# A decoder layer on one core: the third tile's convolution taps move behind the norm of the second output projection, and two weights of the first tile are loaded into a free buffer

## The chip, the core and the metric

The kernel runs on 1 core of one Trainium2 chip. The metric is the time of one execution in microseconds on the device, the median of several runs. Before the change it is 1910.04 us (3 runs, 1907.92 to 1913.49).

The engines go by the profile's names: PE (TensorE, matmuls; PEld is its weight load), DVE (VectorE), ACT (ScalarE), POOL (GpSimd) and SP (SyncE, which issues most DMAs).

## The reference

One hybrid decoder layer, float32, 2048 tokens, width 1024:

```
hn   = rms_norm(x) ; proj = hn @ w_in          # q, k, v and the two halves of a GLU
attn = sliding window attention (window 128, sinks, relative bias)
u    = a * sigmoid(gate)
conv = silu(layer_norm(depthwise causal conv of width 31 (u))) @ w_conv_pw
h    = x + rms_norm(concat(attn, conv) @ w_out)
out  = h + rms_norm((silu(hn2 @ w_gate) * (hn2 @ w_up)) @ w_down),  hn2 = rms_norm(h)
```

## The kernel before

The tokens are cut into 4 tiles of 512 (t = 0 to 3). A float32 product is made as three matmuls of split operands: every operand is a high half, made by a copy on ACT, and a low half, operand minus high half, made by a subtraction on DVE. `split_w` (L130) does this for weights, `split_f` and `lo` for the FFN. A matmul with 512 columns is the unit of PE's work; 24 of them make one unit of the input projection, 12 one product of the FFN.

The stages are generators:

- `stage_a(t)` is the input projection of a tile, in units of 128 output columns. In the first tile units 0 to 3 go together (`four`), and the norm's factor `rb` is multiplied in behind the product (`post`). Units come in GLU pairs (0/1, 2/3, 4/5, 6/7), then k (8), v (9) and q (10 to 13). `proj(u)` loads the weight of unit u through `kweight` (L146) and `weight` (L140) into a tile tagged "raw" (2 buffers; L143 is the load), splits it into two "w" tiles (6 buffers; L133 is the ACT copy, the low half is a DVE subtraction) and runs 24 matmuls. `glu` makes tanh on ACT (L377), the products on DVE, and in the first tile one more multiply by `rb`, on POOL for the first pairs (L385), then stores to `glu_scr`.
- `row_norms` loads the rows of x of the next tile (L276, tag "p"), squares them on ACT (L277) and makes their factors on DVE and POOL.
- `stage_taps(t)`, lane items T0 to T3, is the convolution: 4 channel groups, each loaded from `glu_scr` (L594, L596), one first multiply and 30 taps on DVE (`fc@C<-glu@C,colt,fc@C` in the profile), stored to `y_scr` (L621).
- `stage_b(t)` is the attention of a tile: scores (`tr@B<-kz,ql@A`), masking and row maxima on DVE (L493, L496), exponentials on ACT, transposes and the product with v.
- `stage_w(w)` is the output projection of a tile, for w = 0 and 1 as 32 pieces of 6 matmuls (`mm@W<-w@W,hl@W`); operands `hl@W` are split on ACT (L785) and DVE. `norm_w` is its norm and residual. For w = 1 it is handed to a lane as the item "N1".
- `stage_h_plain` and `stage_h_sums` ("S0") make the FFN's operands, `stage_pre` the first part of the first FFN matrices (products P0.0, P0.1, ...), `stage_p1` the rest and `stage_p2` the down projection. The last two are a Strassen-like scheme of 7 products for 8.

The main sequence is `run(...)` of one stage after another. After every piece of it, `run` lets the lanes emit side work: each lane earns credit (the piece's cost times the lane's rate) and spends it on the costs its generators yield. `lc` is the lane of the taps: T2 has the rate RC2 = 0.4, and each tap costs 0.68. `lh` is the lane of B11.0, B21.0, N1 and S0, at 1.2 for N1. `lc.hold` is a function; while it is true, the lane emits nothing. A tap is also tied behind the last DVE instruction of the main work (`paced`), and its lane has a lower priority (LC = 100). Below this, a planner orders the instructions of each engine by readiness in a timeline of its own and by priority, which is by default the order of emission; buffers of a tag are handed on when their last reader is done. On the chip each engine runs its list in that order.

Before the change T2 is emitted beside `stage_w(1)`, and from the end of `stage_w(1)` the hold is on until S0 is done (S0 starts at product P0.22, `PRE_S0`). The tile "yt" (one buffer of 128 x 2048 float32) is used by the weight join (`stage_join`, from the third tile on), by `stage_tail` and in the FFN; nothing uses it in the first tile.

Of the kernel before, what the change touches and what calls it, by code (L numbers as in the profile page):

```python
# [25 lines left out]
P = 128  # L26
T = 512
# [10 lines left out]
def layer_kernel(ctx, tc, x, xT, cols, rows, sinks, relb, onehot, w_in, w_four, w_pw, w_out, w_gate, w_up, w_down, out):  # L38
    nc = tc.nc
# [9 lines left out]
    def nm(s):  # L49
        uid[0] += 1  # L50
        return f"{s}@{lab[0]}_{uid[0]}"
# [3 lines left out]
    def t_(tag, shape, dt=F32):  # L55
        return sb.tile(list(shape), dt, tag=tag, name=nm(tag), bufs=BUFS[tag])

    def f4(tag, shape=(P, D)):
        return t_(tag, shape)

    def f2(tag, shape=(P, T)):
        return t_(tag, shape)

    def hl(tag):
        return t_(tag, (P, 2, T), F32R)
# [5 lines left out]
    def bank(tag, bufs):  # L71
        return ps.tile([P, T], F32, tag=tag, name=nm(tag), bufs=bufs)

    mm = lambda: bank("mm", 4)
# [65 lines left out]
    def weight(src, low, made, raw=None, on_pool=True):  # L140
        if raw is None:
            raw = t_("raw", (P, 2, T))
            nc.sync.dma_start(raw, src)  # L143
        return [split_w(raw[:, n], "w", low[n], made, on_pool) for n in range(2)]

    def kweight(u, made, raw=None):  # L146
        hs = weight(w_in[u].rearrange("p (a b) -> p a b", a=2), lo_in[u], made, raw, False)
        return [(hs[k // 4][:, 0, (k % 4) * P : (k % 4 + 1) * P], hs[k // 4][:, 1, (k % 4) * P : (k % 4 + 1) * P]) for k in range(KC)]
# [41 lines left out]
    def three(o, pairs, first=True, last=True):  # L190
        n = 3 * len(pairs)
        i = 0
        for (sh, sl), (mh, ml) in pairs:
            for a, b in ((sh, mh), (sh, ml), (sl, mh)):
                mat(o, a, b, start=first and i == 0, stop=last and i == n - 1)
                i += 1
# [58 lines left out]
    started = set()  # L255
# [60 lines left out]
    def split_x(t, xs, rb, ks):  # L316
# [12 lines left out]
            hn.append(hk)  # L329
        return hn  # L330

    def stage_a(t, hn, done_with, hooks, post=None):
        L = f"A{t}"
        lab[0] = L
        rb = None

        def proj(u, bank_of=mm):
            w = kweight(u, t > 0)
            o = bank_of()
            for k in range(KC):  # L340
                three(o, [(w[k], (hn[k][:, 0], hn[k][:, 1]))], k == 0, k == KC - 1)
            return o
# [64 lines left out]
        done_with("S")  # L407
        lab[0] = L
        ok = proj(8)
        if t:  # L410
            act(kz[:, :, 0:P], kz[:, :, T : T + P].bitcast(F32), AF.Copy)
# [212 lines left out]
    def stage_tail(t, sink=None):  # L624
        L = f"C{t}"
        lab[0] = L
        yt = t_("yt", (P, 4, 4 * P))
        ycs = []
        turn = turner(yt, ycs)
        for c in range(4):  # L630
            lab[0] = L
            y = f2("fc")
            nc.sync.dma_start(y, y_scr[c, :, t * T : (t + 1) * T])
            ycs.append(y)
            turn(c)
            yield 0.5
        yield from conv_tail(t, yt, sink)
# [34 lines left out]
    def spare_tile():  # L672
        if not spare:
            spare.append(t_("mb", (P, 2, T)))
        return spare[0]
# [76 lines left out]
    def block_half(acc, units, n, first, L, bank_of, s0=0):  # L752
        cs = slice(n * T, (n + 1) * T)
        for i in range(len(acc)):
            s = i + s0
            lab[0] = L
            o = bank_of()
            three(o, [((a[s // 4][:, 0, ss(s)], a[s // 4][:, 1, ss(s)]), (w[:, 0], w[:, 1])) for a, w in units])
            if first:
                act(acc[i][:, cs], o, AF.Copy)  # L760
            else:
                vtt(acc[i][:, cs], acc[i][:, cs], o, ALU.add)
            yield 0.65 * len(units)

    def load_gb(row):
        gb = []
        for n in range(2):
            t = f2("gb")
            nc.sync.dma_start(t, rows[row, n * T : (n + 1) * T].partition_broadcast(P))
            gb.append(t)  # L770
        return gb
# [6 lines left out]
    def stage_w(w, spill, G, atag, htag, mtag, bank_of, norm=None):  # L778
        L = f"W{w}"
        lab[0] = L  # L780
        acc = [f4(atag) for _ in range(4)]

        def operand(m):
            a = hl(htag)
            act(a[:, 0], m, AF.Copy)  # L785
            vtt(a[:, 1], m, a[:, 0].bitcast(F32), ALU.subtract)
            return [a]

        def acts(gi, ms=None):
            return [operand(m) for m in ms or load(gi)]  # L790

        conv = []
        tail = stage_tail(w, lambda v: conv.append(operand(v))) if w > 1 else ()
        for y in tail:
            if y == YL2:
                break
            yield y
        lab[0] = L

        stage = spare_tile() if w == 1 else None  # L800

        def load(gi):
            ms = []
            pair_ = stage if w == 1 else t_("chl", (P, 2, T)) if w else t_("wx", (P, 2, T)) if gi == 0 else None
            for c in range(G * gi, G * gi + G):
                ms.append(pair_[:, c % 2] if pair_ is not None else f2(mtag))
                nc.sync.dma_start(ms[-1], mixT[c, :, w * T : (w + 1) * T])
            return ms

        first = load(0)  # L810
        gb = load_gb(0) if w > 1 else None
        if w != 1:
            yield 5.0 if w == 0 else 8.0
            lab[0] = L
        nxt = acts(0, first)
        for gi in range(KC // G):
            if w > 1 and G * gi == 4:
                yield from tail
                lab[0] = L
            aa = nxt if w < 2 or G * gi < 4 else conv[G * gi - 4 : G * gi - 4 + G]  # L820
            for n in range(2):
                lab[0] = L
                more = gi + 1 < KC // G and (w < 2 or G * gi + G < 4)
                if n == 0 and more:
                    if w < 2 and G * gi + G == 4:
                        ld.until(f"C{w}")
                        lab[0] = L
                    rows_next = load(gi + 1)
                if n == 1 and more:
                    nxt = acts(gi + 1, rows_next)  # L830
                src = w_out[2 * gi : 2 * gi + 2] if gi < 2 else w_join[2 * gi - 4 : 2 * gi - 2]
                ws = weight(src[:, :, n * T : (n + 1) * T].rearrange("c p t -> p c t"),
                            lo_out[n, 2 * gi : 2 * gi + 2], w > 0, on_pool=False)
                yield from block_half(acc, list(zip(aa, ws)), n, gi == 0, L, bank_of)
        last = norm_w(w, spill, acc, mtag, gb)
        if norm:
            norm(last)
        else:
            yield from last
# [381 lines left out]
    def stage_p2(ws, am, td, last=False):  # L1221
# [34 lines left out]
        def split(i):  # L1256
            if i < len(steps):
                lab[0] = L
                b = split_f(rawb[i], hl(("ql" if i >= len(steps) - 4 else "w") if last else "hl"))
                lo(rawb.pop(i), b, False)  # L1260
                if last and i == len(steps) - 2:
                    rest.append(t_("yt", (P, 2, 2, T), F32R))
                a = split_f(rawa[i], rest[0][:, i % 2] if last and i >= len(steps) - 2 else hl("hl"))
                lo(rawa.pop(i), a, False)
                opsd[i] = a, b
# [79 lines left out]
        for i in range(nn):  # L1345
# [3 lines left out]
            if i + N < nn + (LAST > 0):  # L1349
                split(i + N)  # L1350
            if last and nn - EARLY - 3 <= i < nn - EARLY + LAST - 4:
                load(i + EARLY + 4)
            if last and nn - EARLY <= i < nn - EARLY + LAST - 1:
                split(i + EARLY + 1)
            for b in range(4):
# [33 lines left out]
    def since(lane, name, dt):  # L1389
        return name in lane.done and clk[0] >= lane.done[name] + dt  # L1390
# [66 lines left out]
    PRE_S0, PRE_S2 = 22, 16  # L1457
    H1, H2, H3, H4 = 0, 4, 7, 11
    NH = 24
    EARLY = 12  # L1460
    JL, JS = 10, 2
    lb = Lane(RB, 0)
    lc = Lane(RC0, LC)
    lw = Lane(RW0, 0)
    lf = Lane(1.2, 0)
    lh = Lane(1.2, 0)
# [7 lines left out]
    def run(gen):  # L1474
        for c in gen:
            clk[0] += c
            for lane in lanes:
                lane.pump(c)
# [62 lines left out]
    ws, ops = (0, 1), {}  # L1541
    for n, off in (("B11", 0), ("B21", 4)):
        lh.add(n + ".0", stage_h_plain(ws, ops, n, off), lambda: since(lw, "W0", NH))
    run(stage_w(1, True, 2, "mid", "hl", "at", mm, norm=lambda g: lh.add("N1", g)))
    lc.hold = lambda: "S0" not in lh.done
    lh.add("S0", stage_h_sums(ws, ops), lambda: f"P0.{PRE_S0}" in started and "B3" in lb.done)
    run(stage_pre(ws, ops, mids[0], keeps[0]))
    lt.add("TS", stage_tsums(td))
# [81 lines left out]
```

## Time and profile before

| | us |
|---|---|
| runs: lowest, median, highest | 1907.92, 1910.04, 1913.49 |
| the profiled execution, its time | 1913.71 |
| its span (first to last instruction) | 1912.0 |
| PE busy | 1889.1 |
| DVE busy | 1498.7 |
| ACT busy | 968.6 |
| POOL busy | 200.7 |
| mean granted TensorE clock | 0.999 |

The first tile's input projection runs from 6.2 to about 92 us, the second output projection from 461 to 527, the first FFN product starts at 527.4. A timeline row of the profile reads: start, length, engine, line, operation, output<-inputs, and in brackets the engine's idle time before it with what ended it. A row of the waits reads: who waited for whom, microseconds in total, times, the longest one. L85 is the line of a helper that emits every DVE operation, and L108 that of the matmuls, so rows are told apart by their tiles: the part before @ is the buffer's tag, the letter after it the stage that made it.

### The profile page before, as it was taken

What the parts mean: (1) busy time and instruction counts of PE and PEld (TensorE: products, weight loads), DVE (VectorE), ACT (ScalarE), POOL (GpSimd) and SP (SyncE); (2) the same over time, 40 slices, a digit from 0 to 9 for tenths busy, and PEclk for the clock granted to TensorE, in tenths of its full rate; (3) what the DMA queues carried; (4) which work ended last, traced back from release to release, by engine and by line L of the source; (5) the groups of instructions that cost most, each with busy time, mean ns of one, the idle gap of its engine ahead of it and who ended that gap; (6) DMA issues with size and microseconds to landing.
All of it is one profiled execution on the core that took longest, in us unless ns stands there. A gap on an engine that the chain in (4) does not pass through costs nothing.

```text
span 1912.0 us, 26682 instructions
## 1 busy us (share of the span) xinstructions
PE 1889.1 (99%) x8714; PEld 1530.7 (80%) x8714; DVE 1498.7 (78%) x2806; ACT 968.6 (51%) x1912; POOL 200.7 (10%) x247
## 2 busy tenths in 40 slices
PE   9999999999999999999999999999999999999998
PEld 7777777777778888887888888888888888888886
DVE  6999999998876999988999866787566665455558
ACT  5365445667567433433446583676443343345452
POOL 2010001210000000000000100010033233211002
PEclk9999999999999999999999999999999999999999
DMA  9886756769678776786696696798554543376663
GB/s 334 305 279 231 243 178 188 232 228 344 208 243 288 245 259 237 255 272 222 193 314 205 202 342 204 252 329 313 179 176 151 163 138 127 116 255 188 206 218 130
DMA packets 227644, 439.36 MB, mean 230 GB/s; under 512 B 22664, under 2 KB 48688, under 8 KB 227504
## 3 DMA queue, kind: packets, MB, share of 16 engines
q1 hardware_dynamic: 206192, 403.04, 63.5%
q10 hardware_dynamic: 19392, 28.32, 4.1%
q0 software_dynamic: 1920, 6.29, 0.9%
q8 instruction: 68, 1.11, 0.2%
q14 instruction: 72, 0.59, 0.1%
HBM read 318.54 MB, written 119.02 MB: 229 GB/s over the span
## 4 chain that ended last, share of the span: by engine, by line
PE 72%; DVE 14%; DMA 8%; issue 3%; ACT 1%; POOL 1%; SPq 1%; DVEq 0%; ACTq 0%; POOLq 0%
PE mm@F L108 38%; PE mm@G L108 19%; PE mm@A L108 6%; DVE fc@C L85 5%; PE tr@W L108 4%; PE mm@W L108 2%; PE tr@B L108 1%; DMA glu@C<-glu_scr 1%; DVE sm@G L85 1%; DMA chl@F<-w_gate 1%; DVE w@F L85 1%; DMA p@X<-w_four 1%; DVE tr@B L493 1%; DVE p@B L496 1%; DMA p@A<-x 1%
## 5 line engine op out<-in xcount | busy, mean ns | idle before, releaser
L85 DVE SCALAR_TENSOR_TENSOR fc@C<-glu@C,colt,fc@C 128x512 f32<-128x512 f32 x480 | 353.0, 752 | 1.6
L108 PE MATMUL mm@F<-hl@H,w@F 128*128 128x512 f32 x1056 | 254.4, 390 | 0.0
L108 PEld LDWEIGHTS mm@F<-hl@H,w@F 128*128 128x128 f32 x1056 | 197.9, 188 | 41.9 <-ACT fa@F L1049 0.8
L108 PE MATMUL mm@G<-hl@G,hl@G 128*128 128x512 f32 x924 | 227.6, 393 | 0.1
L891 ACT ACTIVATE w@F<-chl@F 128x512 fp32r<-128x512 f32 x220 | 135.6, 625 | 134.5 <-PE mm@F L108 128.9
L108 PE MATMUL mm@G<-w@G,hl@G 128*128 128x512 f32 x876 | 199.8, 389 | 0.6 <-DVE w@G L85 0.6
L108 PEld LDWEIGHTS mm@G<-hl@G,hl@G 128*128 128x128 f32 x924 | 171.3, 188 | 36.2 <-ACT hl@G L891 0.5
L108 PE MATMUL mm@A<-hl@A,w@A 128*128 128x512 f32 x792 | 193.3, 394 | 1.9 <-DVE w@A L85 1.7
L108 PEld LDWEIGHTS mm@G<-w@G,hl@G 128*128 128x128 f32 x876 | 164.3, 188 | 35.3 <-DVE w@G L85 1.0
L108 PEld LDWEIGHTS mm@A<-hl@A,w@A 128*128 128x128 f32 x792 | 146.6, 188 | 35.3 <-DVE w@A L85 2.2
L85 DVE TENSOR_TENSOR w@F<-chl@F,w@F 128x512 fp32r<-128x512 f32 x198 | 145.6, 739 | 32.7 <-ACT w@F L891 32.2
L108 PE MATMUL mm@F<-ql@H,w@F 128*128 128x512 f32 x528 | 130.4, 391 | 1.8 <-ACT w@F L891 1.4
L108 PE MATMUL mm@F<-mid@H,w@F 128*128 128x512 f32 x528 | 130.2, 390 | 0.0
L108 PE MATMUL mm@F<-p@H,w@F 128*128 128x512 f32 x528 | 129.2, 389 | 0.0
L108 PE MATMUL mm@F<-x@H,w@F 128*128 128x512 f32 x528 | 128.0, 391 | 0.0
L108 PEld LDWEIGHTS mm@F<-ql@H,w@F 128*128 128x128 f32 x528 | 98.4, 188 | 24.0 <-ACT w@F L891 2.3
L108 PEld LDWEIGHTS mm@F<-p@H,w@F 128*128 128x128 f32 x528 | 99.0, 188 | 20.8 <-ACT at@F L1149 0.4
L108 PEld LDWEIGHTS mm@F<-x@H,w@F 128*128 128x128 f32 x528 | 98.6, 188 | 21.1 <-issue 0.8
L108 PEld LDWEIGHTS mm@F<-mid@H,w@F 128*128 128x128 f32 x528 | 99.0, 188 | 20.5
L85 DVE TENSOR_TENSOR w@G<-raw@G,w@G 128x512 fp32r<-128x512 f32 x72 | 50.7, 705 | 67.5 <-ACT w@G L891 66.8
L108 PE MATMUL mm@W<-w@W,hl@W 128*128 128x512 f32 x384 | 97.9, 398 | 2.8 <-DVE hl@W L85 2.1
L133 ACT ACTIVATE w@A<-raw@A 128x512 fp32r<-128x512 f32 x104 | 63.0, 625 | 67.4 <-DMA raw@A<-w_in 38.4
(319 smaller groups left out, 3190.7 us busy)
## 6 DMA issues: line engine op xcount, KB each, us to landing
mids<-fa@F SPq DMA_DIRECT2D x154, 256.0 KB, 2.9
raw@A<-w_in SPq DMA_DIRECT2D x52, 512.0 KB, 5.6
w@A<-lo_in SPq DMA_DIRECT2D x84, 256.0 KB, 4.8
fa@G<-mids SPq DMA_DIRECT2D x74, 256.0 KB, 4.5
fc@G<-mids SPq DMA_DIRECT2D x72, 256.0 KB, 3.6
w@W<-lo_out SPq DMA_DIRECT2D x48, 256.0 KB, 5.0
chl@F<-w_gate SPq DMA_DIRECT2D x22, 512.0 KB, 4.0
raw@F<-w_gate SPq DMA_DIRECT2D x22, 512.0 KB, 4.3
```

The lines of the kernel that those rows point to most:

```text
L85: r = op(*args, **kw)
L108: r = nc.tensor.matmul(*args, **kw)
L133: act(w[:, 0], raw, AF.Copy)
L493: nc.vector.copy_predicated(os[g][:, :, P:], upper.unsqueeze(1).to_broadcast([P, 2, P]), prev)
L496: read = nc.vector.tensor_tensor_reduce(out=pr[:, h], in0=os[g][:, j, P:], in1=bias[0][:, h], op0=ALU.add, op1=ALU.max, scale=1.0, scalar=NEG,
L891: act(w[:, 0], x, AF.Copy)
```

## The change

In the first tile the weights of units 6 and 7 are loaded into the two halves of a "yt" tile and no longer into "raw" buffers. The hold of the tap lane is now true from the first piece of `stage_w(1)` (HW = 0) until N1 is done, and again from the start of product P0.20 until S0 is done; between them T2 is emitted beside `stage_pre`.

```diff
+    early_raw = []
+
     def stage_a(t, hn, done_with, hooks, post=None):
...
         def proj(u, bank_of=mm):
-            w = kweight(u, t > 0)
+            raw = None
+            if post and u in (6, 7):
+                if u == 6:
+                    early_raw.append(t_("yt", (P, 2, 2, T)))
+                raw = early_raw[0][:, u - 6]
+                nc.sync.dma_start(raw, w_in[u].rearrange("p (a b) -> p a b", a=2))
+            w = kweight(u, t > 0, raw)
             o = bank_of()
...
     NH = 24
+    HW = 0
     EARLY = 12
...
-    run(stage_w(1, True, 2, "mid", "hl", "at", mm, norm=lambda g: lh.add("N1", g)))
-    lc.hold = lambda: "S0" not in lh.done
+    held = []
+
+    def second():
+        for i, c in enumerate(stage_w(1, True, 2, "mid", "hl", "at", mm, norm=lambda g: lh.add("N1", g))):
+            if i == HW:
+                held.append(True)
+            yield c
+
+    lc.hold = lambda: (held and "N1" not in lh.done) or (f"P0.{PRE_S0 - 2}" in started and "S0" not in lh.done)
+    run(second())
     lh.add("S0", stage_h_sums(ws, ops), lambda: f"P0.{PRE_S0}" in started and "B3" in lb.done)
```

## The prediction

> **What bounds the kernel now.** I read the page's busy line and chain first, then the waits of PE longest first, then PE's timeline around each wait, and last the timelines of the engines that ended them.
>
> ```profile
> PE 1889.1 (99%) x8714; PEld 1530.7 (80%) x8714; DVE 1498.7 (78%) x2806; ACT 968.6 (51%) x1912; POOL 200.7 (10%) x247
> ...
> PE 72%; DVE 14%; DMA 8%; issue 3%; ACT 1%; POOL 1%; SPq 1%; DVEq 0%; ACTq 0%; POOLq 0%
> ```
>
> PE is the bound: it is busy 1889.1 of 1912.0 us, so at most 22.9 us can be won by removing waits, and the change adds or removes no matmul. The waits of PE, and the last stretch of the windows (its columns: stretch, its length, then busy time of PE, PEld, DVE, ACT, POOL):
>
> ```profile
> PE tr@B L108 <- DVE sm@B L496: 2.8, 3, 1.1
> PE mm@W L108 <- DVE hl@W L85: 2.1, 1, 2.1
> PE mm@A L108 <- DVE w@A L85: 1.7, 1, 1.7
> PE ct@X L108 <- POOL ident masks.py:199: 1.6, 1, 1.6
> ```
> ```profile
> 1800.00:1912.00 112.00, 103.48 (x455) 84.83 (x453) 77.30 (x162) 46.47 (x92) 11.25 (x8) 0.98 0.54 176
> ```
>
> Of the 22.9 us, 1.6 lie before the first matmul and 112.00 - 103.48 = 8.52 in the last stretch; neither is touched. Some 12.7 us remain, in waits of 0.2 to 2.1 us. The longest one on the second output projection (hl@W) and the only long one in the first tile (w@A) are where the change works.
>
> **Part 1: the weights of units 6 and 7.** PE, then DVE, ACT, POOL and SP around that wait:
>
> ```profile
> 41.55 0.73 PE L108 MATMUL mm@A<-hl@A,w@A 128*128 128x512 f32 x2
> 44.03 6.19 PE L108 MATMUL mm@A<-hl@A,w@A 128*128 128x512 f32 x26 [1.74 <-DVE w@A L85]
> ```
> ```profile
> 37.15 0.58 DVE L85 TENSOR_SCALAR sm@A<-sm@A 128x4 f32<-128x4 f32 x3 [1.13 <-ACT junk L277]
> 37.63 0.69 DVE L85 TENSOR_TENSOR fa@A<-mm@A,gb@A 128x512 f32<-128x512 f32 x1
> ...
> 41.62 0.68 DVE L85 TENSOR_TENSOR fa@A<-tr@A,gb@A 128x512 f32<-128x512 f32 x1
> 42.22 1.76 DVE L85 TENSOR_TENSOR w@A<-raw@A,w@A 128x512 fp32r<-128x512 f32 x1
> ```
> ```profile
> 35.96 1.06 ACT L277 ACTIVATE junk<-p@A 128x1024 bf16<-128x1024 f32 x1 [0.67 <-DMA p@A<-x]
> ...
> 37.02 0.58 ACT L313 ACTIVATE gb@A<-ct@A 128x512 f32<-128x512 f32 x1
> ...
> 40.88 1.14 ACT L133 ACTIVATE w@A<-raw@A 128x512 fp32r<-128x512 f32 x2
> ```
> ```profile
> 42.16 1.26 POOL L385 TENSOR_TENSOR fa@A<-fa@A,gb@A 128x512 f32<-128x512 f32 x1
> ```
> ```profile
> 19.98 0.33 SPq L143 DMA_DIRECT2D raw@A<-w_in  x1
> ...
> 24.22 0.49 SPq L276 DMA_DIRECT2D p@A<-x  x1
> ...
> 30.69 0.33 SPq L143 DMA_DIRECT2D raw@A<-w_in  x1
> ```
>
> Unit 6 starts at 41.55, runs two matmuls with the high half of its weight and stops for the low half, which DVE makes at 42.22 to 43.98. Its high half is made at 40.88, behind the tanh chain of the GLU, because its raw weight is asked for only at 30.69: both "raw" buffers were taken by units 4 and 5 (unit 5's load is at 19.98). With the free "yt" tile, the loads of units 6 and 7 have nothing to wait for and can go right behind 19.98. The largest time from issue to landing of these loads is 24.22 to 35.96, under 12 us, so unit 6's weight is there by about 32, and 1.14 us of ACT and two subtractions of DVE then fit well before 41.55. The gain is the whole wait, **-1.74 us**. What is late next is the bank: unit 6 needs the first GLU bank, which the DVE product at 37.63 frees at 38.32, so 3.2 us ahead. Unit 7's two splits move in the same way and save PE nothing, since it doesn't wait for them. With each split moves the store of its low half on SP (L137), of which the waits of SP's queue in the first 75 us say:
>
> ```profile
> SPq L137 <- DVE w@A L85: 17.0, 11, 6.4
> ```
>
> A store that stands there for DVE holds up the loads behind it; two units' stores moved up stand for less, as their subtractions come earlier, and what is behind them are units 8 and up, 10 us and more ahead of PE: at nothing.
>
> Units 8 and 9 find the two raw buffers two units earlier. No later wait is added: the tile's next user, the weight join, starts two tiles on.
>
> Of the 1.76 us of that subtraction 1.07 are more than the 0.69 that the neighbouring product takes, and POOL's multiply runs from 42.16 to 43.42 beside it. [...]
>
> **Part 2: the hold during the second output projection.** PE, DVE and ACT around its two waits:
>
> ```profile
> 505.70 0.98 PE L108 MATMUL tr@B<-kz,ql@A 64*128 64x256 f32 x12 [1.10 <-DVE sm@B L496]
> ...
> 512.52 3.06 PE L108 MATMUL mm@W<-w@W,hl@W 128*128 128x512 f32 x12 [2.10 <-DVE hl@W L85]
> ```
> ```profile
> 505.57 0.07 DVE L496 DVE_READ_ACCUMULATOR2_ANT sm@B<- 128x1 f32 x1
> ...
> 511.79 1.28 DVE L85 TENSOR_TENSOR hl@W<-mb@J,hl@W 128x512 fp32r<-128x512 f32 x2
> ```
> ```profile
> 506.34 1.13 ACT L785 ACTIVATE hl@W<-mb@J 128x512 fp32r<-128x512 f32 x2
> ```
>
> The windows of DVE for all its work and, in the second fence, for the taps alone (stretch, length, busy, count):
>
> ```profile
> 499.00:512.00 13.00, 13.00 (x31) 1.00 0.54 181
> ```
> ```profile
> 461.00:527.00 66.00, 14.35 (x20) 1.00 0.71 242
> 499.00:512.00 13.00, 4.99 (x8) 1.00 0.54 181
> 527.00:561.00 34.00, 7.35 (x9) 1.00 0.78 269
> ...
> 639.00:793.00 154.00, 45.53 (x62) 1.00 0.75 246
> ```
>
> From 499 to 512 DVE is never idle, and 4.99 of its 13.00 us are taps. Both waits end on DVE there: the scores wait for the last read of the block before (505.57), the projection for the low half of its operand (511.79). Without the taps DVE is up to 4.99 us earlier, more than 1.10 + 2.10 = 3.20. What is late next: the operand's high half ends on ACT at 507.47, two subtractions of 1.28 end by 508.75, and PE, after the first gain, wants it at 510.42 - 1.10 = 509.32. So both waits go: **-3.20 us**, between 0 (other work on DVE slides in) and 3.20.
>
> The taps come back elsewhere. By the code's own pacing numbers the projection's 32 pieces of 1.3 at rate 0.4 and 0.68 a tap are some 24 taps; the norm takes 28.1/1.2 = 23.4, or 8.5 products of 2.76, so the lane reopens at the tenth product and closes at the twenty-first: 11 x 2.76 x 0.4 / 0.68 = 18 taps. Counting twelve matmuls a product from the first one, that is 555 to 588 on the chip (all engines):
>
> ```profile
> 555.00:588.00 33.00, 33.00 (x148) 26.05 (x147) 15.84 (x32) 23.08 (x40) 1.76 (x2) 1.00 0.76 264
> 639.00:793.00 154.00, 153.60 (x678) 126.82 (x677) 148.86 (x242) 61.17 (x108) 0.00 (x0) 1.00 0.75 246
> ```
>
> A tap costs 45.53/62 = 0.734 us, 18 are 13.2, and DVE is busy 15.84 of 33: 29.0 of 33, so they lie beside PE and I cost them at **0**. If that cover is gone, the price is what a tap cost PE beside the projection, 3.20/20 = 0.16 us, together 2.9. The other taps, 24 - 18 = 6 by the pacing and 20 + 9 - 18 = 11 by the records, go behind the sums of the operands, into the last stretch quoted, between 0 and 11 x 0.734 = 8.1 us. I take 0, since PE stands only 0.40 us there although DVE is 97% busy, and since the lane is paced: more taps lengthen it, they don't thicken it.
>
> Moved with the taps are their DMAs on SP:
>
> ```profile
> 531.99 0.40 SPq L621 DMA_DIRECT2D y_scr<-fc@C  x1
> ...
> 589.09 0.38 SPq L887 DMA_DIRECT2D fc@H<-hn_scr  x1
> ...
> 792.90 0.32 SPq L621 DMA_DIRECT2D y_scr<-fc@C  x1
> ```
>
> The store of the second channel and the load behind it (531.99) come near 589, just ahead of the loads for the operand sums. If SP had to wait there for a late tap, the FFN weights would queue behind; with DVE under 90% I cost it at nothing. The third tile ends at 792.90; nothing asks for it before the end of the first FFN stage, 100 us on.
>
> **Sum.** -1.74 - 3.20 = -4.94 us. The profiled run took 1913.71 us (span 1912.0 and 1.7 around it), so it would take 1908.8. It lies 3.7 above the median of the runs, 1910.04; carried over to the median the forecast is **1905.1 us**. All instructions are ordered anew by the planner, so waits elsewhere will change by some tenths either way.
>
> **Rivals.**
>
> *The loads push the x rows.* The glu chain starts when the copy at 37.02 is done, and that stands on ACT behind the square at 35.96, which waited for rows issued at 24.22. DMA is full there:
>
> ```profile
> 18.00:36.00 18.00, 18.00 (x87) 14.71 (x86) 10.05 (x30) 8.19 (x15) 2.25 (x3) 1.00 1.04 404
> ```
>
> Two loads of 0.524 MB ahead of it take 2 x 524/404 = 2.6 us at its 404 GB/s, and the chain comes 2.6 us later. The free bank is 3.2 us early, so alone this costs nothing; but if the split still stands behind the chain on DVE, the wait grows to 4.3, and the sum is +2.6 - 3.2 = -0.6: 1909.4. [...] Chance 0.08.
>
> *The waits beside the projection stay*, because the planner puts other DVE work where the taps were, or the moved taps cost their 0.16 us each. Then only part 1 remains: 1908.3. For it: DVE still has 13.00 - 4.99 = 8 us of work in those 13. Chance 0.11.
>
> *The change doesn't do what it says in the first tile*: the planner leaves the split where it is. -3.20 alone: 1906.8. Chance 0.06.
>
> *The squeeze behind the operand sums (slower).* If DVE, 148.86 of 154 us busy there, is what PE stands on as soon as taps are added, each costs its 0.734 us. From 4.94/0.734 = 7 taps on the change loses; with all 11 it is +8.1 - 4.9 = +3.2: 1913.2, and more if the third tile's end pushes the fourth's into the next stage. Against it: PE's 153.60 of 154. Chance 0.20, most of it, 0.16, further out than 0.3% with the reordering on top.
>
> **How the numbers follow.** The runs before lie from 1907.92 to 1913.49, so about 0.3%, 5.7 us, is what a measurement of this kernel can tell from no change; the bounds are 1904.3 and 1915.8. The forecast has 0.55. It stands just inside the lower bound, and its own range, 1902 to 1908, covers it: 0.32 below, where some of the other 12.7 - 4.94 = 7.8 us of waits fall well too, 0.23 above. Of the rivals 0.08, 0.09, 0.06 and 0.04 stay within 0.3%; slower are 0.16 of the squeeze and 0.02 of the second rival with its 2.9 us and new waits on top. Faster 0.32, same 0.23 + 0.27 = 0.50, slower 0.18. The range goes from 1905.1 less 2.1 (median to lowest run) and 1.5 for small waits elsewhere, 1901.5, to the squeeze and 1.3 more, 1914.5; about 0.1 is left out on either side.
>
> **What would show it.** Right: no idle above 0.3 us ahead of unit 6 and none from 500 to 515; no tap between the projection's start and its norm's end; loads of units 6 and 7 right behind unit 5's; DVE near 29 of 33 us from 555 to 588 with PE full. Wrong: the square of the x rows late by some 2.6 us with PE waiting on unit 6; PE idle of several us between 640 and 900; or SP standing on the tap store near 589.

## The result and the profile after

| kernel | median (lowest to highest), us | runs | ratio to before, 95% interval |
|---|---|---|---|
| before, beside it | 1908.45 (1903.53 to 1913.67) | 20 | |
| after | 1914.31 (1909.81 to 1919.66) | 20 | 1.0029 (1.0021 to 1.0037) |

The change makes the kernel slower by 5.9 us. The profiled execution of after took 1912.34 us, with a span of 1910.6. The page of after, its busy line and its shares of the chain:

```profile
PE 1890.3 (99%) x8714; PEld 1535.3 (80%) x8714; DVE 1499.6 (78%) x2806; ACT 969.7 (51%) x1912; POOL 196.6 (10%) x247
...
PE 86%; DVE 7%; DMA 4%; ACT 1%; issue 1%; POOL 0%; SPq 0%; DVEq 0%; ACTq 0%; POOLq 0%
```

PE is as busy as before and the shares look better: DVE ended 14% of the chain and ends 7% now. Taken alone, this page would be read as a gain, but the shares are no measure here: in two more profiles of the same kernel before, DVE ends 8% and 5%. Both stretches that the forecast names are shorter. The timelines of PE and SP of after in the first tile:

```profile
37.65 4.49 PE L108 MATMUL tr@A<-hl@A,w@A 128*128 128x512 f32 x19
41.98 10.36 PE L108 MATMUL mm@A<-hl@A,w@A 128*128 128x512 f32 x45
```
```profile
20.51 0.47 SPq L143 DMA_DIRECT2D raw@A<-w_in  x1
...
23.44 0.85 SPq L345 DMA_DIRECT2D yt@A<-w_in  x2
```

The two loads into "yt" follow unit 5's, and unit 6 runs without the 1.74 us of idle time: the first tile ends at 90.06 and ended at 91.80. That this is the forecast to the hundredth is luck: in the second profiles of both kernels (below) the difference is 91.63 - 90.47 = 1.16. The windows of DVE in after for the taps alone (stretch, length, busy, count):

```profile
499.00:512.00 13.00, 0.00 (x0) 1.00 0.75 227
...
550.00:595.00 45.00, 13.38 (x19) 1.00 0.89 310
```

No tap is left beside the waits at 505 and 512 us, and 19 lie where the forecast put 18. Fifteen taps, emitted before the hold begins, still run from 461 to 480 us, where the forecast expected none. The second output projection takes 63.2 us, before 66.4: -3.2, as was forecast, but not all of it is waiting. PE stood for 3.20 us in it before and stands for 1.81 now, which is 1.4; the rest is work of PE that now lies in other stages. What came in their place stands in PE's timeline of after, with a normal row for comparison at 499.67:

```profile
362.85 5.41 PE L108 MATMUL mm@W<-w@W,hl@W 128*128 128x512 f32 x16 [2.50 <-ACT fa@A L387]
...
383.14 1.12 PE L613 MATMUL ct@C<-ident,fc@C 128*128 128x128 f32 x4 [2.52 <-ACT yt@C L614]
383.91 3.51 PE L108 MATMUL mm@W<-w@W,hl@W 128*128 128x512 f32 x9
...
499.67 3.79 PE L108 MATMUL mm@W<-w@W,hl@W 128*128 128x512 f32 x16
...
821.96 4.32 PE L108 MATMUL mm@F<-ql@H,w@F 128*128 128x512 f32 x12 [2.28 <-ACT mm@F L1143]
826.07 1.87 PE L108 MATMUL mm@F<-mid@H,w@F 128*128 128x512 f32 x6
```

There are three waits of 2.3 to 2.5 us; before had one over 1.75. And the work behind each is slow: the 16 matmuls at 362.85 take 5.41 us, the same 16 at 499.67 take 3.79. That is 1.6 us beside the wait itself, and it doesn't show as idle time, because PE counts as busy: 3.14 of the 3.41 us from 362.58 on, at a granted clock of 0.50.

The first two waits come from ACT, which stands for a DMA and has PE's copy right behind. ACT of after:

```profile
361.68 0.63 ACT L793 ACTIVATE hl@W<-fa@W 128x512 fp32r<-128x512 f32 x1 [6.01 <-DMA fa@W<-mixT]
362.22 0.58 ACT L387 ACTIVATE fa@A<-mm@A 128x512 f32<-128x512 f32 x1
...
381.97 0.63 ACT L133 ACTIVATE w@A<-raw@A 128x512 fp32r<-128x512 f32 x1 [7.35 <-DMA raw@A<-w_in]
382.51 0.58 ACT L614 ACTIVATE yt@C<-ct@C 128x512 f32<-128x512 f32 x1
...
821.31 0.60 ACT L1143 ACTIVATE mm@F<-gb@F 128x512 f32<-128x512 f32 x1 [3.68 <-DMA gb@F<-keeps]
```

The third is the copy of a kept product (`keeps`, made by `stage_pre` and loaded back by `fetch` in `stage_p1`). SP around that load, first before, then after:

```profile
811.10 0.33 SPq L1132 DMA_DIRECT2D fa@F<-mids  x1
811.54 0.36 SPq L1072 DMA_DIRECT2D raw@F<-w_up  x1
812.00 0.38 SPq L1163 DMA_DIRECT2D mids<-fa@F  x1
812.43 0.42 SPq L1104 DMA_DIRECT2D gb@F<-keeps  x1
```
```profile
808.68 0.33 SPq L1140 DMA_DIRECT2D fa@F<-mids  x1
809.06 0.42 SPq L1204 DMA_DIRECT2D td<-wx@G  x1
...
810.05 0.43 SPq L1082 DMA_DIRECT2D chl@F<-w_gate  x1
811.27 0.33 SPq L629 DMA_DIRECT2D y_scr<-fc@C  x1
811.65 0.70 SPq L604 DMA_DIRECT2D glu@C<-glu_scr  x1
812.54 1.12 SPq L1204 DMA_DIRECT2D td<-wx@G  x1
813.71 0.78 SPq L1171 DMA_DIRECT2D mids<-fa@F  x1
814.54 0.50 SPq L1112 DMA_DIRECT2D gb@F<-keeps  x1
```

The row at 811.27 is the last store of the third tile; before it stood at 792.90. It now lies with a load of the fourth tile (811.65) between the load of `mids` and that of `keeps`, which comes 5.9 us behind the former and came 1.3 behind it. Of these 4.5 us the two rows take 1.0, and SP stands 0.7 for the last tap ahead of them; the rest is for the most part other rows that the new order put there (two stores to `td`, a load of `w_gate`) and SP's own waits.

### The profile page after: what moved, and what is told of

Read it like the earlier page. It is cut to its first block, busy times and chain, and to the rows that moved or that the text cites. A ratio compares the mean times of both kernels' runs of the same rounds, so it can differ in the third digit from the quotient of the medians.

```text
span 1910.6 us, 26656 instructions
## 1 busy us (share of the span) xinstructions
PE 1890.3 (99%) x8714; PEld 1535.3 (80%) x8714; DVE 1499.6 (78%) x2806; ACT 969.7 (51%) x1912; POOL 196.6 (10%) x247
## 4 chain that ended last, share of the span: by engine, by line
PE 86%; DVE 7%; DMA 4%; ACT 1%; issue 1%; POOL 0%; SPq 0%; DVEq 0%; ACTq 0%; POOLq 0%
PE mm@F L108 43%; PE mm@G L108 19%; PE mm@A L108 11%; PE tr@W L108 5%; PE mm@W L108 3%; DVE fc@C L85 2%; PE tr@B L108 2%; DMA raw@A<-w_in 1%; DVE sm@G L85 1%; DMA raw@W<-w_out 1%; PE ct@J L108 1%; PE tr@B L546 1%; PE tr@A L108 1%; PE tr@H L917 1%; DVE x@G L85 0%
```

## The experiments

**Theory.** Each part wins what was forecast and is paid for elsewhere: the first part by ACT's order before the second output projection (363, 383 us), the second by the end of the third tile on SP (822 us), and each wait over some 2 us costs clock on top. **Rivals:** the moved taps fill DVE (the squeeze of the prediction); or the planner's dealing anew (its ordering all instructions again after any edit) costs by itself, whatever is changed.

Where a kernel was profiled, five numbers are compared, from PE's timeline (us): the end of the first tile, the start of the second output projection, of the first FFN stage and of the down projection, and the length of that FFN stage.

| | tile 1 | out 2 | FFN 1 | down | FFN 1 length |
|---|---|---|---|---|---|
| before | 91.80 | 460.93 | 527.36 | 956.77 | 429.4 |
| before again (e4) | 91.63 | 460.54 | 528.12 | 956.76 | 428.6 |
| before, third time (e14) | 96.23 | 463.04 | 527.46 | 955.57 | 428.1 |
| null (e10) | 92.12 | 461.80 | 527.06 | 953.15 | 426.1 |
| first part alone (e1) | 89.63 | 463.01 | 525.47 | 956.74 | 431.3 |
| unit 6 alone (e8) | 89.14 | 456.13 | 524.83 | 955.16 | 430.3 |
| after | 90.06 | 462.51 | 525.68 | 956.97 | 431.3 |
| after again (e3) | 90.47 | 461.55 | 523.59 | 958.04 | 434.5 |
| hold alone (e2) | 91.88 | 458.34 | 527.48 | 960.47 | 433.0 |
| unit 6 and hold (e15) | 89.86 | 456.17 | 527.70 | 963.58 | 435.9 |
| null and hold (e16) | 91.37 | 461.30 | 529.72 | 963.42 | 433.7 |

A stage's length also holds the side work that the lanes put into it, so that it is no price by itself. The second table has what is lost: PE's idle time (length less busy time), and the steps of 3.41 us in which the granted clock was half, each of which loses half its length, 1.7 us (shown under "What a wait costs"). "Lost" is idle time and 1.71 us a step.

| | up to out 2: idle, us | steps | lost, us | out 2 to down: idle, us | steps | lost, us |
|---|---|---|---|---|---|---|
| before | 7.6 | 0 | 7.6 | 5.7 | 0 | 5.7 |
| before again (e4) | 7.8 | 0 | 7.8 | 4.6 | 1 | 6.3 |
| before, third time (e14) | 6.7 | 2 | 10.1 | 2.2 | 0 | 2.2 |
| null (e10) | 8.5 | 0 | 8.5 | 1.8 | 0 | 1.8 |
| first part alone (e1) | 8.2 | 2 | 11.6 | 4.5 | 0 | 4.5 |
| unit 6 alone (e8) | 4.6 | 0 | 4.6 | 8.4 | 0 | 8.4 |
| after | 6.7 | 2 | 10.2 | 4.1 | 1 | 5.8 |
| after again (e3) | 5.9 | 2 | 9.3 | 5.6 | 1 | 7.3 |
| hold alone (e2) | 5.3 | 0 | 5.3 | 9.1 | 3 | 14.2 |
| unit 6 and hold (e15) | 4.2 | 0 | 4.2 | 12.0 | 4 | 18.8 |
| null and hold (e16) | 7.8 | 0 | 7.8 | 9.8 | 2 | 13.2 |

### The parts alone

The first part alone, without the hold:

```diff
...
-    lc.hold = lambda: (held and "N1" not in lh.done) or (f"P0.{PRE_S0 - 2}" in started and "S0" not in lh.done)
-    run(second())
+    run(stage_w(1, True, 2, "mid", "hl", "at", mm, norm=lambda g: lh.add("N1", g)))
+    lc.hold = lambda: "S0" not in lh.done
```

> Only the two early weights of the first tile; the hold is that of before. Theory A (the early loads make the planner order everything up to the second output projection anew, and the new order waits longer beside the first output projection): first tile's wait of 1.7 us gone, but waits of 2 us and more between 340 and 400 us with slow matmuls behind them; 3 to 8 us slower than before. Theory B (the moved taps cost the time, after 527 us): 1 to 2 us faster than before.

Measured: 1.0018 (1.0008 to 1.0029). The two long waits are there, 3.24 us at 362.92 and 2.82 at 383.59, so they belong to the first part. The 1.74 us won in the first tile are given back before the second output projection, which starts at 463.0 (before: 460.9). The waits of 1.10 and 2.10 us that the hold was to remove are gone here already, although eight taps still lie beside them. DVE of this kernel, the taps alone:

```profile
499.00:512.00 13.00, 6.03 (x8) 1.00 0.61 202
```

The hold alone, on the first tile of before:

```diff
-            if post and u in (6, 7):
-                if u == 6:
-                    early_raw.append(t_("yt", (P, 2, 2, T)))
-                raw = early_raw[0][:, u - 6]
-                nc.sync.dma_start(raw, w_in[u].rearrange("p (a b) -> p a b", a=2))
...
```

> Only the hold of the taps; the first tile is that of before. Theory A: the waits of 1.1 and 2.1 us beside the second output projection shrink as forecast, nothing new up to 460 us; 2 to 4 us faster than before. Theory B: 3 to 7 us slower than before, with new waits of PE between 555 and 900 us.

Measured: 1.0043 (1.0026 to 1.0061), no less than both parts together. The wait for the kept product is there (2.45 us at 825.43), and another that after has only as 0.78 us: 3.97 at 507.40, where the transposes of the FFN operand wait for a copy on ACT. From the second output projection to the down projection this kernel loses 14.2 us, and before lost 2.2 to 6.3: the hold alone wins nothing there.

The change once more, and before once more:

> The changed kernel once more, for a second look at where it waits. Both theories: about 1.003 of before. Theory A: the waits at about 360 and 383 us and the slow matmuls behind them come again, and longer than in the first look where the run is slower. Theory B: they don't differ from before's, and the waits after 527 us do.

Measured: 1.0029 (1.0017 to 1.0041), with waits at the same three places (2.99 us at 363.51, 1.25 at 383.69, 3.96 at 822.00).

> The kernel before once more, for a second look: its profiled execution was 5 us above its median. Both theories: ratio 1.000. Theory A: beside the first output projection its waits stay below 2 us and no matmul behind them is slow.

Measured: 0.9998 (0.9985 to 1.0011). The wait at 512 us is as long as in the first profile, 2.10, but this time the same twelve matmuls behind it took 4.31 us, not 3.06. PE of before again:

```profile
511.71 4.31 PE L108 MATMUL mm@W<-w@W,hl@W 128*128 128x512 f32 x12 [2.10 <-DVE hl@W L85]
```

The weight of unit 6 alone in the free buffer, without the hold:

```diff
-            if post and u in (6, 7):
+            if post and u == 6:
```

> Only unit 6 of the first tile has its weight in the free buffer; the hold is that of before. Theory A (the early loads deal the order from there on anew, and the loss sits beside the first output projection by the luck of that order): the wait of 1.7 us at unit 6 is gone as with both units, and the waits between 300 and 460 us are others than with both units, better or worse. If instead the early load as such costs the time, half of the loss remains: about 1.001 of before.

Measured: 1.0016 (1.0006 to 1.0026). The wait of the first tile is gone here too, and so are the long waits at 363 and 383: they come from the order that both weights bring, not from the load of unit 6. The time is still not below before, so those waits are not the whole cost of the first part: PE stands for 4.9 us in the first FFN stage (before: 1.2 to 2.5), in waits of up to 1.51.

The same with the hold:

> The change with the weight of unit 6 alone in the free buffer, that of unit 7 in raw as before: another order up to the second output projection, without the long waits at 363 and 383 us (as in the run of unit 6 alone). Theory 'two costs, each at its place': those waits are gone, the wait for the kept product near 822 us stays, 0.15 to 0.35% slower than before at a clock between those of the two. Rival 'the waits come with any dealing of the first part': long waits between 350 and 390 us again, 0.3% or more.

Measured: 1.0040 (1.0027 to 1.0053); against unit 6 alone the hold costs again (18.8 us lost from the second output projection to the down projection, and 8.4 without it). It has both waits of the hold alone: 3.44 us at 508.30 and 3.26 at 827.53.

### Is it the dealing anew?

The null: before with a tenth warm-up matmul ahead of the first unit.

```diff
-    NWARM = 9
+    NWARM = 10
```

> The kernel before with 10 instead of 9 matmuls of 128x128 ahead of the first unit (about 0.1 us, in PE's start wait). It has no part of the change and takes away no wait, but the planner deals the order anew. Theory 'dealing anew costs by itself': 0.1 to 0.4% slower than before, waits of PE of 1 to 3 us at places that have nothing to do with the start. Rival 'the change's own edits cost': within 0.1% of before.

Measured: 1.0006 (0.9997 to 1.0016). The order differs, as its waits do (1.09 us at 366.52, 1.32 at 369.26, 1.05 at 509.72; those of 2.1 at 512 and 1.05 at 873 are gone), and the time doesn't. So another order need not cost 0.3%. This is one order, though, and not a proof for all: the control of the next section, which only moves some loads to another issuing engine, is 0.28% slower than before, and three of the four edits of after there are 0.39 to 0.64% slower than after.

The hold on the order of the null:

```diff
...
-    lc.hold = lambda: "S0" not in lh.done
+    lc.hold = lambda: (held and "N1" not in lh.done) or (f"P0.{PRE_S0 - 2}" in started and "S0" not in lh.done)
```

> The kernel of the null run (a tenth warm-up matmul, 1.0006 of before) with the hold of the change and without its first part. Theory 'the hold itself costs at the third tile's end': 0.2 to 0.45% slower than before, the third tile ends near 811 to 816 us and a wait of 2 us or more for the kept product follows. Rival 'the hold's cost was a bad dealing': within 0.15% of before, no such wait, although the third tile ends as late.

Measured: 1.0065 (1.0053 to 1.0077). The same two waits at the same two places. PE, ACT and SP of this kernel:

```profile
510.36 0.78 PE L909 MATMUL ct@H<-ident,fa@H 128*128 128x128 f32 x4 [3.97 <-ACT chl@H L929]
...
828.64 4.39 PE L108 MATMUL mm@F<-ql@H,w@F 128*128 128x512 f32 x12 [3.25 <-ACT mm@F L1135]
```
```profile
509.06 0.19 ACT L516 ACTIVATION_READ_ACCUMULATOR p@B<-p@B,sm@B 128x1 f32 x1
509.16 0.58 ACT L539 ACTIVATE p@B<-tr@B 128x512 f32<-128x512 f32 x1
509.63 0.67 ACT L929 ACTIVATE chl@H<-ct@H,colt 128x512 f32<-128x512 f32 x1
```
```profile
815.62 0.33 SPq L1132 DMA_DIRECT2D fa@F<-mids  x1
...
818.18 0.33 SPq L621 DMA_DIRECT2D y_scr<-fc@C  x1
818.55 0.43 SPq L596 DMA_DIRECT2D glu@C<-glu_scr  x1
...
821.12 0.47 SPq L1104 DMA_DIRECT2D gb@F<-keeps  x1
```

On three orders of the work (before's, unit 6's, the null's) the hold alone brings the same pair: the copy of the FFN operand on ACT stands behind a row of exponentials (509.06 is the last), and the kept product's load stands behind the third tile's last store. With the hold 13.2 to 18.8 us are lost from the second output projection to the down projection, without it 1.8 to 8.4 on the same orders. Both parts together avoid the first of them (0.78 us at 508.04), which fits with after being no slower than the hold alone.

### The end of the third tile

Four kernels, and a control, were to move what meets at 822 us. The loads of the kept products of the first FFN on POOL, in after and, as a control, in before:

```diff
-                nc.sync.dma_start(kept[m], keep[m])
+                (nc.sync if ws[0] else nc.gpsimd).dma_start(kept[m], keep[m])
```

> The changed kernel, with the loads of the kept products in the first FFN stage issued from POOL, which has nothing to do there, and not from SP. Theory C (the third tile now ends near 815 us, and its store and the next tile's load stand on SP ahead of a load of a kept product, for which ACT and then PE wait, and the clock drops behind that wait): no wait of PE and no slow matmuls near 822 us, 3 to 5 us faster than the changed kernel, so 1.000 to 1.002 of before. Theory D (the loss after 527 us is DVE full with moved taps): the same time as the changed kernel, 1.003.

Measured: 1.0049 (1.0033 to 1.0064). The wait at 822 is gone, but the same copy is waited for at 685.48 (1.53 us) and 759.35 (1.98).

> The kernel before, with the same loads issued from POOL. Control for the first run: before has no wait for these loads, so theory C expects 1.000; if it is as much faster as the first run is than the changed kernel, the move helps by itself and says nothing of the change.

Measured: 1.0028 (1.0016 to 1.0039): the control is slower too, with waits for that copy at 778.17 (1.69) and 807.44 (1.77). So the pair says only that the load's moment decides; it doesn't price the wait.

A faster lane for the third tile, so that it ends earlier:

```diff
+    lc.rates["T2"] = 0.44
```

> The changed kernel, with the third tile's taps at 0.44 and not 0.40 from the first FFN stage on, so that the tile ends near 795 us as before. Theory C: the wait near 822 us is gone as in the run beside it, 1.000 to 1.002 of before, unless the end meets another load. Theory D: DVE is fuller and the kernel slower than the changed one, 1.004 and more.

Measured: 1.0074 (1.0057 to 1.0091). The wait at 822 is gone; others are at 892.84 (3.46), 1109.19 (2.05) and 1217.06 (2.39).

The hold for the second half of the projection only:

```diff
-    HW = 0
+    HW = 16
```

> The change with the hold from the sixteenth of the 32 pieces of the second output projection on (HW = 16), so that about half of the 19 taps stay beside it. Theory 'third tile's end': the taps end earlier, nearer to 803 us than to 811, and the wait for the kept product at 822 us with its slow matmuls (about 3.7 us together) is gone or shorter; the waits at 363 and 383 us, which belong to the first part, stay. Time 1909 to 1912, against 1914. Rival 'moved taps fill DVE': the same direction, half of the hold's own cost. Rival 'dealing anew': no relation, 1908 to 1918.

Measured: 1.0093 (1.0078 to 1.0109), a miss. The waits at 363 and 383 stay (1.79, 2.36), that at 822 is gone as expected, though the third tile ended at 762 and not near 803. But PE waits in the down projection, at 1208.22 (1.37), 1210.78 (1.91) and 1223.69 (1.74), and behind it at 1324.26 (3.03).

Two DMAs on POOL:

```diff
-            nc.sync.dma_start(y_scr[c, :, t * T : (t + 1) * T], y)
+            (nc.gpsimd if (t, c) == (2, 3) else nc.sync).dma_start(y_scr[c, :, t * T : (t + 1) * T], y)
...
-            nc.sync.dma_start(g, glu_scr[c, :, t * T - HALO : (t + 1) * T])
+            (nc.gpsimd if (t, c) == (3, 0) else nc.sync).dma_start(g, glu_scr[c, :, t * T - HALO : (t + 1) * T])
```

> The change, with only two DMAs issued by POOL and not by SP: the store of the third tile's last channel and the first load of the fourth tile. Theory 'the third tile's end stands on SP ahead of the kept product': the wait at 822 us (2.28) and the matmuls at half speed behind it (1.4 us) go or shrink, and nothing else changes up to 811 us; 2 to 4 us less in the profile, 0.1 to 0.2% in the time. Rival 'the kept product comes late because its buffer comes free late': the wait stays at 2 us or more.

Measured: 1.0068 (1.0052 to 1.0084), a miss in the time. The store left SP (POOL has it at 811.74) and the wait at 822 is gone; but the load that was moved is one of 712 us, and the one behind the store (812.31) is the fourth tile's second, still on SP. The planner dealt the stage anew: the down projection starts at 968.25, with 3.78 us of waiting at 898.58.

In these four the wait at 822 goes when the third tile's end or the load leaves its place, and in the kernels of the tables it is there in all five profiles with the hold and in none of the six without it. So its local cause is shown, as far as edits can show it that also deal the stage anew. None shows the time without it, since each made new waits of 1.5 to 3.8 us; in after DVE is busy 388.25 of the 431.29 us of the first FFN stage.

### What a wait costs

Bursts of matmuls with waits between them, nothing else:

> Nothing of the layer is computed: bursts of 36 to 51 matmuls 128x512 of the kernel's own form, and after each a wait of PE for a chain of ACT copies whose length goes from about 1 to about 5 us in thirty steps, three times over. Theory 'a wait costs its length': behind every wait the matmuls run at once at their normal 0.22 us. Theory 'a wait also costs clock': behind waits up to about 2.0 us they run normally, behind some of 2.1 to 2.5 and behind most of the longer ones they take about 0.43 us each for the next 2 to 7 us, so that such a wait costs 1.3 to 3 us more than its length.

No result on the question: matmuls of later bursts were put in ahead of each wait, and it shrank to under 0.25 us. Only the last, 4.60 us, stayed.

Mended, so that each burst reads what the chain writes:

```diff
+    r = h
...
-                    nc.tensor.matmul(o, w[:, 0:P], h, start=True, stop=True)
+                    nc.tensor.matmul(o, w[:, 0:P], r, start=True, stop=True)
...
```

> Nothing of the layer is computed. As the run of waits before, where matmuls were put in ahead of the waits; now each burst of 36 to 51 matmuls 128x512 reads what the chain of ACT copies writes, so that PE must stand for the whole chain: about 1 to 5 us in thirty steps, three times over. Theory 'a wait costs its length': behind every wait the matmuls run at their normal 0.22 us at once. Theory 'a wait also costs clock': none is slow behind waits up to about 2.0 us, some behind 2.1 to 2.5, most behind 3 and more; slow ones take about 0.43 us each for some microseconds, so that the burst is 1.3 to 3.5 us longer than its normal length.

PE of this kernel, some of 89 bursts (length, and how many matmuls, then the wait ahead of it):

```profile
103.14 10.04 PE L60 MATMUL mm@M<-r@M,w 128*128 128x512 f32 x43 [1.80 <-ACT r@M L65]
115.06 10.76 PE L60 MATMUL mm@M<-r@M,w 128*128 128x512 f32 x39 [1.88 <-ACT r@M L65]
...
155.29 8.93 PE L60 MATMUL mm@M<-r@M,w 128*128 128x512 f32 x38 [2.38 <-ACT r@M L65]
...
271.21 11.22 PE L60 MATMUL mm@M<-r@M,w 128*128 128x512 f32 x48 [3.28 <-ACT r@M L65]
...
377.22 14.06 PE L60 MATMUL mm@M<-r@M,w 128*128 128x512 f32 x50 [4.36 <-ACT r@M L65]
```

At 0.2334 us a matmul (10.04/43) the second burst should take 9.10 and takes 10.76. Over all bursts, length less 0.2334 a matmul:

| wait, us | bursts | of them slow | lost beside the wait, us |
|---|---|---|---|
| 0.97 to 1.80 | 24 | 0 | 0 |
| 1.87 to 1.96 | 6 | 4 | 1.6 |
| 2.29 to 2.62 | 15 | 9 | 1.4 to 1.7, once 2.9 |
| 2.96 to 3.28 | 15 | 11 | 1.5 to 1.7, twice 2.7 to 2.9 |
| 3.62 to 4.60 | 29 | 29 | 1.4 to 1.7, ten times 2.1 to 2.9 |

So in the bursts a wait up to 1.80 us cost its length, and a longer one mostly 1.6 us more. The long waits of the layer kernel lost the same amount: 5.41 - 3.79 = 1.62 at 362.85, and (4.32 - 3.02) + (1.87 - 1.52) = 1.65 at 821.96 by the lengths of undisturbed rows of twelve and of six. Of the 36 waits of 1.87 to 3.28 us, 24 were followed by slow matmuls, so the length of the wait alone doesn't decide.

The clock itself stands in the windows of a profile, whose columns here are stretch, length, PE's busy time and matmuls, granted clock, DMA share and GB/s. Around 362.85 in after, then around the wait of 2.10 us in before and in before again:

```profile
359.17:362.58 3.41, 1.18 (x6) 1.00 0.80 256
362.58:365.99 3.41, 3.14 (x7) 0.50 0.46 135
365.99:369.41 3.42, 3.42 (x16) 1.00 0.10 38
```
```profile
510.80:514.22 3.42, 1.70 (x7) 1.00 0.73 216
514.22:517.63 3.41, 3.41 (x18) 1.00 0.43 165
```
```profile
509.72:513.14 3.42, 1.43 (x6) 1.00 0.71 206
513.14:516.55 3.41, 3.41 (x12) 0.50 0.47 180
```

The clock goes to half for whole steps of 3.413 us, which lose 1.7 us of work each. In every profile these steps begin a multiple of 3.413 us apart (in after at 362.58, 383.06 and 823.38: 6 and 129 steps), so they lie on a fixed grid and don't start with the wait. What decides is how long PE stands within one step of it. Of the wait of 2.10 us, 3.42 - 1.70 = 1.72 us fell into one step in before, and the clock stayed; 1.99 did in before again, and the next step ran at half. Over all profiles but that of e9, up to the last matmul, 79 steps at full clock were followed by one at half, each with 1.79 us or more of idle PE; of the other steps at full clock none had over 1.91. A step that was itself at half was followed by a second one when PE stood in it for 0.61 us or more (19 times), and not at 0.49 or less (79 times). So a step need not be idle throughout: some 1.9 of its 3.413 us were enough for the next one to run at half.

Before, a third time:

> The kernel before once more, for a third profiled execution: the two profiled so far took 1913.7 and 1913.2 us, 5 above the median of its runs, so that the profiles alone show no difference to the change. Theory 'the first FFN stage of before has no long wait': the first FFN product to the first product of the down projection takes 428 to 430 us again, no matmuls at half speed behind a wait there, at any total time from 1905 to 1914. Rival 'before has the change's waits too in some executions': 431 us or more there.

Measured: 1910.95 in that execution. The FFN stage took 428.1 and no wait over 1 us lies in it. But the first tile cost more, by the clock; PE of this execution, by rows and by steps of the clock:

```profile
43.12 0.73 PE L108 MATMUL mm@A<-hl@A,w@A 128*128 128x512 f32 x2 [0.96 <-ACT w@A L133]
45.58 9.04 PE L108 MATMUL mm@A<-hl@A,w@A 128*128 128x512 f32 x26 [1.74 <-DVE w@A L85]
```
```profile
41.42:44.84 3.42, 1.47 (x6) 1.00 0.61 191
44.84:48.25 3.41, 2.67 (x6) 0.50 0.69 254
48.25:51.66 3.41, 3.41 (x9) 0.50 1.01 241
```

The same 26 matmuls behind the same 1.74 us took 6.19 in the first profile, 2.85 less. The 0.96 us and 1.0 of the 1.74 fell into one step (3.42 - 1.47 = 1.95 us of idle PE), and the rest, 0.74, into the next, which was at half already, so that two steps ran at half.

## Why the prediction was wrong

**Part 1, right in its place.** The 1.74 us went, the loads stand where they were expected, and the rows of x are not pushed: the square on ACT that waits for them starts at 36.09 (before 35.96), 0.13 us later and not 2.6, so that rival falls; no run shows its 2.6 us.

**Part 2, the waits went, but what the hold wins hangs on the order.** The 19 taps lie beside full PE, as forecast, and no PE time is lost from 550 to 595. But the forecast took the 3.20 us as what the hold wins. The first part alone is rid of both waits with the taps still there, so their end in after doesn't show what the hold does. By PE's idle time in the projection, the hold wins 2.3 and 3.2 us on the order of the first part (4.1 without it, 1.8 and 0.9 in after's two profiles). On the three other orders it loses: 4.0 and two steps at half clock against 3.2, 2.8 and one, and 1.0 (before's three profiles), 5.3 and two against 3.6 (unit 6), 4.0 and one against 1.5 (null). The step of the forecast that fails there is "What is late next": it looked at ACT's half of `hl@W` and not at ACT's copy of the FFN operand, for which PE then stood 3.4 to 4.0 us. The squeeze behind the operand sums, the slower rival, gave about the time that came (1913.2), but not for its reason: from 640 to 800 PE of after is busy 160.00 of 160 us.

**The step that failed first: "All instructions are ordered anew by the planner, so waits elsewhere will change by some tenths either way."** In the profiles of after there are new ones of 2.3 to 4.0 us. In the part between the first tile and the second output projection after takes 372.5 and 371.1 us in its two profiles, where before took 369.1, 368.9 and 366.8; e1 and e8 show that the waits at 363 and 383 come with both weights and not with unit 6 alone. PE's idle time in that part is hardly longer (5.1 and 4.2 us, before 4.0, 4.1 and 2.3): it is gathered into few long waits, and these took two steps of the clock, 3.4 us.

**The step that failed second: the third tile "ends at 792.90; nothing asks for it".** True of its data, not of its queue: its last store and the load behind it moved to 811 us on SP, ahead of the kept product. I had looked for its DMAs near 589, where the taps start again, and not where they end. The first FFN stage got 1.9 and 5.0 us longer than the 429.4 of before; with the hold on three other orders 433.0 to 435.9. The first part alone has 431.3 too, but there it is moved work: it loses 0.5 us in this stage to idle time and clock, after 4.0 and 6.5, and before 1.2 to 2.5.

**The step that failed third: a wait was priced at its length.** Each of after's two profiles has three steps at half clock, 5.1 us together; those of before have none, one and two. Every timed run has its mean clock: before has 0.9985 over the 83 runs beside the experiments, after 0.9967 over 20. That is 0.0018 x 1910 = 3.4 us, over half of the 5.9. Among the runs of before alone, those at 0.999 took 1907.8 on average (47 runs), at 0.998 1909.7 (29) and at 0.997 1912.3 (6), so a thousandth is indeed some 2 us.

**A term of the sum that was luck.** The forecast carried a distance of -3.7 us from the profiled execution to the median over to after, where it measured 1914.31 - 1912.34 = +2.0. Of the 9.2 us between 1905.1 and 1914.31, 5.6 are this term; 3.6 are in the profiled execution, 1912.34 against the 1908.8 of the sum.

**Open.** The profiles alone show no loss: before took 1913.71, 1913.16 and 1910.95 in them, after 1912.34 and 1913.97. The profiled executions of before lie 3 to 5 us above the medians of its runs and those of after up to 2 us below its own, for which no experiment gave a reason. So the 2.5 us of the 5.9 that the clock doesn't cover are argued from the waits and not shown. Unit 6 alone, at a clock of 0.9987, is 0.16% slower than before, which the clock doesn't explain either. Why the hold puts the copy of the FFN operand behind the exponentials was not tried. No version tried beats before.

## What to carry to other kernels

When side work is moved later, follow it to its end: the DMAs of its last piece arrive in a queue that others depend on there. Don't sum waits by length alone: once PE stood for some 1.9 us within one 3.41 us step of the clock, the next step cost 1.7 us more, which the profile books as busy time, so removing two short waits and adding one long one can lose. The granted clock of the windows shows it. And measure an order that is dealt anew for no reason (the null, 1.0006) before blaming, or trusting, the planner; one such order is a sample, not a bound.

## What was not expected of the hardware

The price of a wait is a step, not a slope: in the bursts none of 24 waits up to 1.80 us was followed by slow matmuls, all of 29 from 3.62 us were, and between them the same length went free or cost 1.6 us, by where it fell on the grid of 3.413 us. The bound holds for a step and not for a wait: in the third profile of before two waits of 0.96 and 1.74 us, 0.7 us of work apart, cost two steps at half clock. Loads of the kept products issued by POOL and not by SP made before slower by 0.28% (0.16 to 0.39).
